# Two weight sums of a seven-product block made by accumulating loads instead of vector subtractions

## The chip, the core and the metric

The kernel runs on one core of a Trainium2 chip. The metric is the device time of one execution in microseconds (us), as a median over runs. TensorE (PE in the profile) multiplies, PEld is its weight load, VectorE is DVE, ScalarE is ACT, GpSimd is POOL, and SyncE (SP) does nothing but start transfers here. Transfers started by SP and by GpSimd go through queues of their own.

## The reference

One layer of a streaming encoder: a norm, one wide input projection, two mixers, two gated projections, an output projection with a residual sum, and a SwiGLU block, on 256 rows of 2048 in float32.

```python
h = rms_norm(x, norm_mix[l])
proj = jnp.einsum('btd,dn->btn', h, w_in[l])
...
gates = jax.nn.sigmoid(gate_logits + b_gate[l]); gate_a, gate_b = jnp.split(gates, 2, axis=-1)
...
merged = (gate_a * jnp.einsum('btc,cd->btd', y_a, w_proj_a[l])
          + gate_b * jnp.einsum('btc,cd->btd', y_b, w_proj_b[l]))
x = x + jnp.einsum('btd,de->bte', merged, w_out[l])
h = rms_norm(x, norm_ffn[l])
gate_up = jnp.einsum('btd,df->btf', h, w_ffn_in[l])
ff_gate, ff_up = jnp.split(gate_up, 2, axis=-1)
x = x + jnp.einsum('btf,fd->btd', jax.nn.silu(ff_gate) * ff_up, w_ffn_out[l])
```

The weights w_in, w_ffn_in and w_ffn_out are by far the largest arrays, and nearly all of the time is the multiplication with them.

## The kernel before

**Tiles.** A weight matrix lies in memory as blocks of 512 columns by 512 rows: a chunk `kc` of a block `nb` is four k-tiles of 128 rows, each 128 x 512 (256 KB). The 256 rows of activations are two halves, m = 0 and 1. Each operand is split into a high part in float32r and the rest: `hi = copy(w)` on ScalarE, `lo = w - hi` on VectorE. A product is then a triple of matmuls, hi x hi, hi x lo and lo x hi, into one bank. A plain product of one chunk and one block is 4 k-tiles by 2 halves, 8 triples; of a pair of blocks, 16.

**Seven products.** For some chunks of some pairs of blocks, `product_pair` handles the first two k-tiles of the chunk, the two halves of the rows and the two blocks as a 2 x 2 by 2 x 2 block product with seven products instead of eight; the other two k-tiles go plainly, with 8 triples. Such a chunk is called a use here: 7 + 8 = 15 triples. There are 46 uses: four in each of two gate pairs (`SEVEN_GATE`), four in one pair of the output projection (`SEVEN_OUT`), four in each of five FFN pairs (`SEVEN_IN`), and seven (`SEVEN`) of the eleven chunks in each of the two pairs of the last product. Four sums of weights are needed: `weight_forms` makes two of them in `ta` and two in `tb`, each 128 x 512, by four vector instructions, all from line 194 of the profile. `act_forms` makes the four sums of activations; `four_sums` and `residual_sums` put the products together.

**Stages of a weight.** A `fetch` loads two tiles of two k-tiles (512 KB each) from SP's queue into the pool `wraw` of 8 buffers. `halves` splits one raw tile into a `hi` and a `lo` tile, of which there are 4 each; ScalarE and VectorE can thus prepare at most four tiles ahead of TensorE. `ta` and `tb` both come from the pool `t6` of 2 buffers. Within a use the preparation goes: first raw tile, the single k-tile of the second, `ta`, `tb`, then the two raw tiles of the plain part (`early` uses, the first chunk of a product with `plain_first`, have the plain part first). 

**Order.** Loads and splits are traced with a priority 500 instructions ahead (`PREP_AHEAD`). The order of the instructions on each engine is fixed when the program is built, by a list scheduler that works with modelled durations, priorities and free buffers; at run time each engine takes its instructions in that order and waits on semaphores. TensorE's order is as written. Side work (transposes, mixers) comes in through `tick`, every four triples. GpSimd has little to do: loads and stores of `x` and of spilled activation forms, the gate additions of line 809, and small powers for the norms.

Of the kernel before, what the change touches and what calls it, by code (L numbers as in the profile page):

```python
# [10 lines left out]
F32 = mybir.dt.float32  # L11
# [34 lines left out]
def block_kernel(ctx: ExitStack, tc: tile.TileContext, x, x_t, w_in, w_pa, w_pb, w_out, w_fi, w_fo,  # L46
# [51 lines left out]
    def add(out, a, b):  # L98
        nc.vector.tensor_tensor(out=out, in0=a, in1=b, op=ALU.add)

    def rsqrt_mean(dst, ss, n):

        w = ss.shape[-1]
        ms = t_small([P, 8], "ms")
        nc.vector.tensor_scalar(ms[:, :w], ss, 1.0 / n, EPS, ALU.mult, ALU.add)
        nc.gpsimd.tensor_tensor(out=dst, in0=ms[:, :w], in1=neg_half[:, :w], op=ALU.pow)
# [17 lines left out]
    def fetch(w, nb, kc, n=2, pinned=False):  # L124

        res = []
        for hf in range(2):
            raw = wraw_p.tile([P, 2, 512], F32, tag="raw", name=nm("raw"))
            for k in range(0, 2, n):
                d = nc.sync.dma_start(out=raw[:, k:k + n, :],  # L130
                                      in_=w[nb, kc, :, 2 * hf + k:2 * hf + k + n, :])
                if pinned:
                    tc.keep_in_program_order(d)
            res.append(raw)
        return res

    def load_weights(w, nb, kc, n=2, raw=None):

# [46 lines left out]
        split(hi[:, 0:n, :], lo[:, 0:n, :], src)  # L185
        return [(hi[:, k, :], lo[:, k, :]) for k in range(n)]

    def weight_forms(r0, r1):


        ta = t6_p.tile([P, 2, 512], F32, tag="t6", name=nm("ta"))
        tb = t6_p.tile([P, 2, 512], F32, tag="t6", name=nm("tb"))
        b11, b21, b12, b22 = r0[:, 0, :], r0[:, 1, :], r1[:, 0, :], r1[:, 1, :]
        op = lambda out, x, y, o: nc.vector.tensor_tensor(out=out, in0=x, in1=y, op=o)  # L194
        p1, p2 = halves(r0)
        p3, = halves(r1[:, 1:2, :])
        op(ta[:, 0, :], b12, b11, ALU.subtract)
        op(ta[:, 1, :], b22, b12, ALU.subtract)
        p5, p7 = halves(ta)
        op(tb[:, 0, :], ta[:, 0, :], b22, ALU.subtract)  # L200
        op(tb[:, 1, :], b21, tb[:, 0, :], ALU.add)
        p6, p4 = halves(tb)
        return {1: p1, 2: p2, 3: p3, 4: p4, 5: p5, 6: p6, 7: p7}

    def product_pair(w, nbs, n_chunks, act, forms, c_pool, u_pool, epilogue, plain_first=False,
                     last=False):

        tag = {id(mm): "mm", id(aux): "bank"}  # L210
        cb, ub = {}, {}
        count = [0]

        def bank_of(d, key, pool):
            if key not in d:
                d[key] = pool.tile([P, 512], F32, tag=tag[id(pool)], name=nm("mp"))
                return d[key], True
            return d[key], False

        def triple(psb, a, b, final):  # L220
            (ps, first), (ah, al), (wh, wl) = psb, a, b
            nc.tensor.matmul(ps, lhsT=ah, rhs=wh, start=first, stop=False)  # L222
            nc.tensor.matmul(ps, lhsT=ah, rhs=wl, start=False, stop=False)  # L223
            nc.tensor.matmul(ps, lhsT=al, rhs=wh, start=False, stop=final)  # L224
            count[0] += 1
            if count[0] % 4 == 0:
                tick()

        def seven(kc, tf):
            sf = forms[kc]  # L230
            form = {5: 0, 6: 1, 7: 2, 3: 3}
            plain = {1: (0, 0), 2: (1, 0), 4: (1, 1)}
            dest = {2: (0, 0), 3: (0, 1), 4: (1, 0)}
            for p in (1, 2, 3, 5, 7, 6, 4):
                if p in form:
                    a = (sf[:, 0, form[p], :], sf[:, 1, form[p], :])
                else:
                    k, m = plain[p]
                    a = act(kc * 4 + k, m)
                if p in dest:  # L240
                    triple(bank_of(cb, dest[p], c_pool), a, tf[p], False)
                else:
                    triple(bank_of(ub, p, u_pool), a, tf[p], kc == max(forms))
            if kc == max(forms):
                epilogue(ub)

        for kc in range(n_chunks):
            end = kc == n_chunks - 1
            early = plain_first and kc == 0
            with tc.high_priority(offset=min(PREP_AHEAD, tc.cur_priority - first_block[0])):  # L250
                r = [fetch(w, nb, kc) for nb in nbs]
                ws = [[None] * 4 for _ in nbs]
                if kc not in forms:
                    for n in range(2):
                        ws[n][0:2] = halves(r[n][0])
                        ws[n][2:4] = halves(r[n][1])
                else:
                    if not early:
                        tf = weight_forms(r[0][0], r[1][0])
                    for n in range(2):  # L260
                        ws[n][2:4] = halves(r[n][1])
                    if early:
                        tf = weight_forms(r[0][0], r[1][0])
            if kc in forms and not early:
                seven(kc, tf)
            ks = [k for k in range(4) if ws[0][k] is not None]
            order = [(n, k, m) for n in range(2) for k in ks for m in range(2)]
            if last and end:
                order = [(n, k, m) for n in range(2) for m in range(2) for k in ks]
            for n, k, m in order:  # L270
                triple(bank_of(cb, (m, n), c_pool), act(kc * 4 + k, m), ws[n][k], end and k == 3)
            if kc in forms and early:
                seven(kc, tf)
        return cb
# [42 lines left out]

    def act_forms(pt, f, gain=None):

        s = t2([P, 4, P], "sf")  # L320
        a11, a21, a12, a22 = (pt[:, k, m * P:(m + 1) * P] for k in range(2) for m in range(2))

        def op(out, x, k, y, o):
            if gain is None:
                nc.vector.tensor_tensor(out=out, in0=x, in1=y, op=o)
            else:
                nc.vector.scalar_tensor_tensor(out=out, in0=x, scalar=gain[:, k:k + 1], in1=y,
                                               op0=ALU.mult, op1=o)

        if gain is None:  # L330
            nc.scalar.copy(s[:, 2, :], a21)
        else:
            nc.scalar.activation(s[:, 2, :], a21, AF.Copy, scale=gain[:, 0:1])
        op(s[:, 0, :], a22, 1, s[:, 2, :], ALU.add)
        op(s[:, 2, :], a11, 0, s[:, 2, :], ALU.subtract)
        op(s[:, 1, :], a11, 0, s[:, 0, :], ALU.subtract)
        op(s[:, 3, :], a12, 1, s[:, 1, :], ALU.add)
        split(f[:, 0], f[:, 1], s)

    def picker(tiles):  # L340
# [406 lines left out]
    def four_sums(ub, e00, e10, e01, e11):  # L747

        nc.scalar.copy(e00, ub[1])
        add(e01, ub[6], e00)  # L750
        add(e10, ub[7], e01)
        add(e11, ub[5], e10)
        add(e01, ub[5], e01)

    def x_forms():

# [10 lines left out]
    for nb in range(4):  # L767
# [13 lines left out]
        if nb in SEVEN_GATE:  # L781
            def sums(ub):
                for br in range(2):
                    gates[br, nb] = t4([P, 2, 512], "gate")
                four_sums(ub, *(gates[br, nb][:, m, :] for br in range(2) for m in range(2)))

            cb = product_pair(w_in, (14 + nb, 18 + nb), 4, act_x, fq, aux, mm, sums,
                              plain_first=True, last=True)
            for br in range(2):
                gt = gates[br, nb]  # L790
                for m in range(2):
                    add(gt[:, m, :], cb[m, br], gt[:, m, :])
                    nc.vector.scalar_tensor_tensor(out=gt[:, m, :], in0=gt[:, m, :],
                                                   scalar=r1[:, m:m + 1], in1=bgs[br],
                                                   op0=ALU.mult, op1=ALU.add)
                    nc.scalar.activation(gt[:, m, :], gt[:, m, :], AF.Sigmoid)
# [23 lines left out]
    def residual_sums(x0, x1):  # L820
        def sums(ub):
            u2, u3 = t2([P, 512], "u2"), t2([P, 512], "u3")
            add(x0[:, 0, :], x0[:, 0, :], ub[1])
            nc.scalar.copy(u2, ub[1])
            add(u2, ub[6], u2)
            add(u3, ub[7], u2)
            add(x1[:, 0, :], x1[:, 0, :], u2)
            add(x0[:, 1, :], x0[:, 1, :], u3)
            add(x1[:, 1, :], x1[:, 1, :], u3)
            for m in range(2):  # L830
                add(x1[:, m, :], ub[5], x1[:, m, :])
        return sums

    def norm_block(nb, ps):
# [30 lines left out]
    def swiglu_pair(j):  # L865
# [7 lines left out]
        cb = product_pair(w_fi, (j, NJ + j), 4, act_x2, fx, aux, mm, sums, plain_first=True,  # L873
                          last=True)
        for m in range(2):
            add(hn[:, m, :], cb[m, 0], hn[:, m, :])
            nc.scalar.activation(hn[:, m, :], hn[:, m, :], AF.Silu, scale=r2[:, m:m + 1])
        for m in range(2):
            add(u[m], cb[m, 1], u[m])
# [110 lines left out]
```

## Time and profile before

| | us |
|---|---|
| median of 3 runs | 1428.48 |
| lowest and highest run | 1426.71, 1428.92 |
| the profiled execution | 1427.22 |
| its span, first to last instruction | 1425.4 |
| PE busy in the span | 1417.6 |
| DVE busy | 1063.6 |
| ACT busy | 774.2 |
| POOL busy | 50.1 |

The profile is of one execution. Its span leaves out 1.8 us that lie around the first and the last instruction. Busy times are unions of an engine's instructions; a busy PE can still be waiting inside a matmul, so the pace from matmul to matmul is read beside it.

### The profile page before, as it was taken

How to read it: one execution, taken by the hardware profiler on the slowest of the kernel's cores; microseconds unless marked ns; L12 is line 12 of the kernel's file. 1: busy time of each engine (PE TensorE's matmuls, PEld its weight loads, DVE VectorE, ACT ScalarE, POOL GpSimd, SP SyncE). 2: the span in 40 equal slices, each digit the busy share in tenths (PEclk: the TensorE clock that was granted, in tenths of full speed). 3: DMA queues.
4: the chain of work that ended last, by engine and by line, in shares of the span. 5: the costliest groups of instructions: out<-in, count | busy, mean ns of one | idle time of the engine just before them, and what ended most of it. 6: DMA issues, size and time to landing. Idle time of an engine off the chain costs nothing.

```text
span 1425.4 us, 17596 instructions
## 1 busy us (share of the span) xinstructions
PE 1417.6 (99%) x6448; PEld 1174.4 (82%) x6448; DVE 1063.6 (75%) x1361; ACT 774.2 (54%) x1009; POOL 50.1 (4%) x63
## 2 busy tenths in 40 slices
PE   9999999999999999999999999999999999999998
PEld 7888888888888888878888888888788888888887
DVE  6768869564878697689767769687796876777875
ACT  7756565555655454455555546455454554544553
POOL 0100100100000000100000000000000010000000
PEclk9999999999999999999999999999999999999999
DMA  9654354446657556547654657656476578666652
GB/s 360 243 192 161 134 193 156 164 163 195 222 183 240 197 197 210 184 148 239 220 203 168 228 169 240 206 179 228 164 238 206 178 254 303 210 221 221 208 183 84
DMA packets 81848, 288.37 MB, mean 202 GB/s; under 512 B 9185, under 2 KB 9441, under 8 KB 81761
## 3 DMA queue, kind: packets, MB, share of 16 engines
q1 hardware_dynamic: 78272, 274.66, 57.5%
q0 software_dynamic: 3488, 12.58, 2.3%
q8 instruction: 50, 0.82, 0.2%
q14 instruction: 38, 0.30, 0.1%
HBM read 279.34 MB, written 7.86 MB: 201 GB/s over the span
## 4 chain that ended last, share of the span: by engine, by line
PE 98%; DVE 1%; ACT 0%; DMA 0%; issue 0%; SPq 0%; DVEq 0%; ACTq 0%
PE mm L169 18%; PE mm L168 18%; PE mm L170 18%; PE mp L223 13%; PE mp L224 13%; PE mp L222 13%; PE bank L285 2%; PE bank L543 1%; DVE wlo L178 1%; ACT whi L177 0%; PE bank L573 0%; DMA raw<-in_w_in 0%; PE bank L619 0%; PE bank L670 0%; PE bank L698 0%; DVE tb L194 0%
## 5 line engine op out<-in xcount | busy, mean ns | idle before, releaser
L148 DVE TENSOR_TENSOR wlo<-raw,whi 128x1024 fp32r<-128x1024 f32 (+1 forms) x292 | 351.9, 1212 | 175.6 <-ACT whi L147 173.4
L147 ACT CAST whi<-raw 128x1024 fp32r<-128x1024 f32 (+1 forms) x292 | 301.9, 1040 | 292.7 <-PE mm L170 219.8
L178 DVE TENSOR_TENSOR wlo<-raw,whi 128x1024 fp32r<-128x1024 f32 x216 | 235.0, 1110 | 51.9 <-ACT whi L177 50.8
L177 ACT CAST whi<-raw 128x1024 fp32r<-128x1024 f32 x216 | 201.2, 960 | 121.8 <-PE mp L224 59.6
L168 PE MATMUL mm<-whi,xTh 128*128 128x512 f32 x576 | 226.6, 398 | 1.3 <-ACT whi L147 1.3
L169 PE MATMUL mm<-wlo,xTh 128*128 128x512 f32 x576 | 225.2, 391 | 0.0
L170 PE MATMUL mm<-whi,xTl 128*128 128x512 f32 x576 | 225.1, 391 | 0.0
L168 PE MATMUL mm<-whi,x2Th 128*128 128x512 f32 x384 | 150.0, 391 | 0.0
L170 PE MATMUL mm<-whi,x2Tl 128*128 128x512 f32 x384 | 149.5, 389 | 0.0
L169 PE MATMUL mm<-wlo,x2Th 128*128 128x512 f32 x384 | 149.4, 389 | 0.0
L168 PEld LDWEIGHTS mm<-whi,xTh 128*128 128x128 f32 x576 | 108.2, 188 | 23.0 <-ACT whi L147 2.0
L170 PEld LDWEIGHTS mm<-whi,xTl 128*128 128x128 f32 x576 | 108.2, 188 | 22.6
L169 PEld LDWEIGHTS mm<-wlo,xTh 128*128 128x128 f32 x576 | 108.3, 188 | 21.8 <-DVE wlo L148 1.0
L223 PE MATMUL mp<-wlo,hTh 128*128 128x512 f32 x282 | 109.7, 389 | 0.0
L224 PE MATMUL mp<-whi,hTl 128*128 128x512 f32 x282 | 109.6, 389 | 0.0
L222 PE MATMUL mp<-whi,hTh 128*128 128x512 f32 x282 | 99.7, 390 | 0.0
L177 ACT CAST whi<-ta 128x1024 fp32r<-128x1024 f32 x46 | 48.3, 1050 | 89.9 <-PE mp L224 87.4
L178 DVE TENSOR_TENSOR wlo<-ta,whi 128x1024 fp32r<-128x1024 f32 x46 | 56.2, 1223 | 48.3 <-ACT whi L177 48.3
L224 PE MATMUL mp<-whi,x2Tl 128*128 128x512 f32 x220 | 86.2, 392 | 0.0
L223 PE MATMUL mp<-wlo,x2Th 128*128 128x512 f32 x220 | 86.2, 392 | 0.0
L170 PEld LDWEIGHTS mm<-whi,x2Tl 128*128 128x128 f32 x384 | 72.1, 188 | 15.0
L168 PEld LDWEIGHTS mm<-whi,x2Th 128*128 128x128 f32 x384 | 72.1, 188 | 14.8
(256 smaller groups left out, 2260.8 us busy)
## 6 DMA issues: line engine op xcount, KB each, us to landing
raw<-in_w_fi SPq DMA_DIRECT2D x176, 512.0 KB, 4.4
raw<-in_w_in SPq DMA_DIRECT2D x172, 512.0 KB, 4.1
raw<-in_w_fo SPq DMA_DIRECT2D x88, 512.0 KB, 5.3
raw<-in_w_out SPq DMA_DIRECT2D x32, 512.0 KB, 4.3
raw<-in_w_pa SPq DMA_DIRECT2D x16, 512.0 KB, 3.7
raw<-in_w_pb SPq DMA_DIRECT2D x16, 512.0 KB, 4.3
x<-x POOLq DMA_DIRECT2D x8, 512.0 KB, 5.7
kept<-sform POOLq DMA_DIRECT2D x7, 512.0 KB, 4.9
```

The lines of the kernel that those rows point to most:

```text
L147: nc.scalar.copy(hi[:, sl, :], src[:, sl, :])
L148: nc.vector.tensor_tensor(out=lo[:, sl, :], in0=src[:, sl, :], in1=hi[:, sl, :].bitcast(F32), op=ALU.subtract)
L168: nc.tensor.matmul(ps[m], lhsT=ah, rhs=wh, start=kc == 0 and k4 == 0, stop=False)
L169: nc.tensor.matmul(ps[m], lhsT=ah, rhs=wl, start=False, stop=False)
L170: nc.tensor.matmul(ps[m], lhsT=al, rhs=wh, start=False, stop=kc == n_chunks - 1 and k4 == 3)
L177: nc.scalar.copy(hi, src)
L178: nc.vector.tensor_tensor(out=lo, in0=src, in1=hi.bitcast(F32), op=ALU.subtract)
L222: nc.tensor.matmul(ps, lhsT=ah, rhs=wh, start=first, stop=False)
L223: nc.tensor.matmul(ps, lhsT=ah, rhs=wl, start=False, stop=False)
L224: nc.tensor.matmul(ps, lhsT=al, rhs=wh, start=False, stop=final)
L285: nc.tensor.transpose(out=pt[:, j, m * P:(m + 1) * P], in_=nat[:, m, c:c + P], identity=ident)
L543: nc.tensor.matmul(pl[:, j, :], lhsT=ek[:, g // 2, (g % 2) * P:(g % 2 + 1) * P], rhs=eq[:, g, :], start=True, stop=True)
```

## The change

A use no longer fetches its first two k-tiles as two plain raw tiles. `fetch_pair` loads the first k-tile of both blocks into the two halves of a raw tile `ta`, and GpSimd's queue then starts a load of the second block's first two k-tiles into the same tile with an addition (`accum_op`), so that `ta` holds two sums when it lands. It must wait for the two loads. The plain values needed beside it are loaded into two more raw tiles, `b1` and half of `b22`; the plain part's two raw tiles stay as they were. A use thus takes five raw tiles of the eight instead of four. `weight_forms` makes only the two sums of `tb`. All four sums of weights are now additions, so some signs of the products change, and `act_forms`, `four_sums`, `residual_sums` and the callers of the results add where they subtracted and the other way round, with the same number of instructions.

```diff
+    def fetch_pair(w, nbs, kc):
+        ta = raw_tile()
+        for n in range(2):
+            nc.sync.dma_start(out=ta[:, n, :], in_=w[nbs[n], kc, :, 0, :])
+        nc.gpsimd.dma_start(out=ta, in_=w[nbs[1], kc, :, 0:2, :], accum_op=ALU.add)
+        b1, b22 = raw_tile(), raw_tile()
+        nc.sync.dma_start(out=b1, in_=w[nbs[0], kc, :, 0:2, :])
+        nc.sync.dma_start(out=b22[:, 1, :], in_=w[nbs[1], kc, :, 1, :])
+        rest = []
+        for nb in nbs:
+            rest.append(raw_tile())
+            nc.sync.dma_start(out=rest[-1], in_=w[nb, kc, :, 2:4, :])
+        return (ta, b1, b22), rest
...
-    def weight_forms(r0, r1):
-        ta = t6_p.tile([P, 2, 512], F32, tag="t6", name=nm("ta"))
+    def weight_forms(ta, b1, b22):
         tb = t6_p.tile([P, 2, 512], F32, tag="t6", name=nm("tb"))
-        b11, b21, b12, b22 = r0[:, 0, :], r0[:, 1, :], r1[:, 0, :], r1[:, 1, :]
-        op = lambda out, x, y, o: nc.vector.tensor_tensor(out=out, in0=x, in1=y, op=o)
-        p1, p2 = halves(r0)
-        p3, = halves(r1[:, 1:2, :])
-        op(ta[:, 0, :], b12, b11, ALU.subtract)
-        op(ta[:, 1, :], b22, b12, ALU.subtract)
+        p1, p2 = halves(b1)
+        p3, = halves(b22[:, 1:2, :])
         p5, p7 = halves(ta)
-        op(tb[:, 0, :], ta[:, 0, :], b22, ALU.subtract)
-        op(tb[:, 1, :], b21, tb[:, 0, :], ALU.add)
+        add(tb[:, 0, :], ta[:, 0, :], b22[:, 1, :])
+        add(tb[:, 1, :], b1[:, 1, :], tb[:, 0, :])
         p6, p4 = halves(tb)
...
-        if gain is None:
-            nc.scalar.copy(s[:, 2, :], a21)
-        else:
-            nc.scalar.activation(s[:, 2, :], a21, AF.Copy, scale=gain[:, 0:1])
-        op(s[:, 0, :], a22, 1, s[:, 2, :], ALU.add)
-        op(s[:, 2, :], a11, 0, s[:, 2, :], ALU.subtract)
-        op(s[:, 1, :], a11, 0, s[:, 0, :], ALU.subtract)
-        op(s[:, 3, :], a12, 1, s[:, 1, :], ALU.add)
+        nc.scalar.activation(s[:, 3, :], a21, AF.Copy, scale=1.0 if gain is None else gain[:, 0:1])
+        op(s[:, 0, :], a22, 1, s[:, 3, :], ALU.subtract)
+        op(s[:, 2, :], a11, 0, s[:, 3, :], ALU.subtract)
+        op(s[:, 1, :], a11, 0, s[:, 0, :], ALU.add)
+        op(s[:, 3, :], a12, 1, s[:, 1, :], ALU.subtract)
...
-        add(e01, ub[6], e00)
-        add(e10, ub[7], e01)
-        add(e11, ub[5], e10)
-        add(e01, ub[5], e01)
+        sub(e01, ub[6], e00)
+        sub(e10, e01, ub[7])
+        sub(e11, e10, ub[5])
+        sub(e01, e01, ub[5])
```

`residual_sums` and the three places that add the results of a pair get the same kind of edit: a `sub` with the same operands where an `add` stood.

## Rows read from the trace of the kernel before

**Rows 1.** The page's first part: busy us, share of the span, instructions.
```profile
span 1425.4 us, 17596 instructions
...
PE 1417.6 (99%) x6448; PEld 1174.4 (82%) x6448; DVE 1063.6 (75%) x1361; ACT 774.2 (54%) x1009; POOL 50.1 (4%) x63
```

**Rows 2.** The page's chain that ended last, shares by engine.
```profile
PE 98%; DVE 1%; ACT 0%; DMA 0%; issue 0%; SPq 0%; DVEq 0%; ACTq 0%
```

**Rows 3.** Windows: stretch, its length, each engine's busy us, PE clock, DMA share, GB/s.
```profile
0.00:36.00 36.00, 33.53 (x135) 26.41 (x136) 23.64 (x44) 25.58 (x48) 1.76 (x9) 1.00 0.95 361
...
505.00:545.00 40.00, 40.00 (x178) 33.04 (x177) 37.12 (x45) 23.28 (x27) 0.00 (x0) 1.00 0.66 225
...
900.00:940.00 40.00, 40.00 (x182) 33.12 (x181) 25.27 (x32) 19.06 (x23) 0.53 (x1) 1.00 0.56 184
...
1400.00:1425.00 25.00, 21.41 (x95) 17.41 (x93) 15.78 (x20) 7.65 (x8) 0.00 (x0) 1.00 0.11 42
```

**Rows 4.** Timeline of PE inside a use: start us, us, instruction (first and last of nine).
```profile
1249.67 0.39 PE L224 MATMUL mp<-whi,hTl 128*128 128x512 f32 x1
...
1251.48 0.39 PE L224 MATMUL mp<-whi,hTl 128*128 128x512 f32 x1
```

**Rows 5.** Waits of PE's weight loads: us in total, times, longest.
```profile
PEld mp L222 <- ACT whi L177: 3.2, 6, 1.0
PEld mp L223 <- DVE wlo L178: 2.5, 7, 0.5
```

**Rows 6.** The line of the weight sums: ns min/median/max, first and last start.
```profile
L194 DVE TENSOR_TENSOR ta<-raw,raw x46: 682/691/996, 387.6 to 1387.3; 128x512 f32<-128x512 f32 x46
L194 DVE TENSOR_TENSOR ta<-raw x46: 680/685/689, 388.2 to 1387.9; 128x512 f32<-128x512 f32 x46
```

**Rows 7.** Timeline of DVE in the last product, two successive uses.
```profile
1242.34 1.23 DVE L178 TENSOR_TENSOR wlo<-ta,whi 128x1024 fp32r<-128x1024 f32 x1 [2.45 <-ACT whi L177]
1243.60 0.69 DVE L194 TENSOR_TENSOR ta<-raw,raw 128x512 f32<-128x512 f32 x1
1244.20 0.69 DVE L194 TENSOR_TENSOR ta<-raw 128x512 f32<-128x512 f32 x1
...
1252.99 1.22 DVE L178 TENSOR_TENSOR wlo<-ta,whi 128x1024 fp32r<-128x1024 f32 x1 [1.26 <-ACT whi L177]
...
1255.76 1.22 DVE L178 TENSOR_TENSOR wlo<-tb,whi 128x1024 fp32r<-128x1024 f32 x1 [0.21 <-ACT whi L177]
```

**Rows 8.** DMA issues: out<-in, engine, count, KB each, median us to landing.
```profile
raw<-in_w_fo SPq DMA_DIRECT2D x88, 512.0 KB, 5.3
...
raw<-in_w_pa SPq DMA_DIRECT2D x16, 512.0 KB, 3.7
...
x<-x POOLq DMA_DIRECT2D x8, 512.0 KB, 5.7
kept<-sform POOLq DMA_DIRECT2D x7, 512.0 KB, 4.9
sf<-kept POOLq DMA_DIRECT2D x7, 512.0 KB, 10.1
raw<-in_w_in SPq DMA_DIRECT2D x8, 256.0 KB, 6.2
...
bg<-in_b_gate SPq DMA_DIRECT2D x8, 256.0 KB, 4.5
```

**Rows 9.** Timeline of ACT at the same crossing.
```profile
1254.67 1.05 ACT L177 CAST whi<-tb 128x1024 fp32r<-128x1024 f32 x1 [1.72 <-PE mp L224]
```

**Rows 10.** All waits: who waited for whom, us in total, times, longest.
```profile
DVE ta L194 <- DMA raw<-in_w_fi: 8.2, 4, 2.3
```

**Rows 11.** Timeline of POOL: the last gate additions.
```profile
623.22 3.00 POOL L809 TENSOR_TENSOR gate<-gate,gate 128x512 f32<-128x512 f32 x2 [19.29 <-DVE gate L808]
```

**Rows 12.** The tile bank after them: weight loads of its transposes, ns, first and last start.
```profile
L285 PEld LDWEIGHTS bank<-ident,gate x8: 138/138/141, 628.5 to 631.0; 128*128 128x128 f32 x8
```

More of the change, by code (lines that the diff above doesn't have):

```diff
@@ L99, in add, with sub @@
         nc.vector.tensor_tensor(out=out, in0=a, in1=b, op=ALU.add)
+    def sub(out, a, b):
+        nc.vector.tensor_tensor(out=out, in0=a, in1=b, op=ALU.subtract)
     def rsqrt_mean(dst, ss, n):
@@ L127, in fetch @@
         for hf in range(2):
-            raw = wraw_p.tile([P, 2, 512], F32, tag="raw", name=nm("raw"))
+            raw = raw_tile()
             for k in range(0, 2, n):
@@ L135, in fetch, with raw_tile @@
         return res
+    def raw_tile():
+        return wraw_p.tile([P, 2, 512], F32, tag="raw", name=nm("raw"))
+    def fetch_pair(w, nbs, kc):
[11 more added lines that the diff above has]
+        return (ta, b1, b22), rest
     def load_weights(w, nb, kc, n=2, raw=None):
@@ L250, in product_pair @@
             with tc.high_priority(offset=min(PREP_AHEAD, tc.cur_priority - first_block[0])):
-                r = [fetch(w, nb, kc) for nb in nbs]
                 ws = [[None] * 4 for _ in nbs]
                 if kc not in forms:
+                    r = [fetch(w, nb, kc) for nb in nbs]
                     for n in range(2):
@@ L257, in product_pair @@
                 else:
+                    r, rest = fetch_pair(w, nbs, kc)
                     if not early:
-                        tf = weight_forms(r[0][0], r[1][0])
+                        tf = weight_forms(*r)
                     for n in range(2):
-                        ws[n][2:4] = halves(r[n][1])
+                        ws[n][2:4] = halves(rest[n])
                     if early:
-                        tf = weight_forms(r[0][0], r[1][0])
+                        tf = weight_forms(*r)
             if kc in forms and not early:
@@ L791, in block_kernel @@
                 for m in range(2):
-                    add(gt[:, m, :], cb[m, br], gt[:, m, :])
+                    (sub if (m, br) == (1, 0) else add)(gt[:, m, :], cb[m, br], gt[:, m, :])
                     nc.vector.scalar_tensor_tensor(out=gt[:, m, :], in0=gt[:, m, :],
@@ L824, in sums @@
             nc.scalar.copy(u2, ub[1])
-            add(u2, ub[6], u2)
-            add(u3, ub[7], u2)
+            sub(u2, ub[6], u2)
+            sub(u3, u2, ub[7])
             add(x1[:, 0, :], x1[:, 0, :], u2)
-            add(x0[:, 1, :], x0[:, 1, :], u3)
+            sub(x0[:, 1, :], x0[:, 1, :], u3)
             add(x1[:, 1, :], x1[:, 1, :], u3)
             for m in range(2):
-                add(x1[:, m, :], ub[5], x1[:, m, :])
+                sub(x1[:, m, :], x1[:, m, :], ub[5])
         return sums
@@ L875, in swiglu_pair @@
         for m in range(2):
-            add(hn[:, m, :], cb[m, 0], hn[:, m, :])
+            (sub if m == 1 else add)(hn[:, m, :], cb[m, 0], hn[:, m, :])
             nc.scalar.activation(hn[:, m, :], hn[:, m, :], AF.Silu, scale=r2[:, m:m + 1])
```

## Prediction

> **What bounds the kernel now.** I read the first lines of the page first: TensorE has work in 1417.6 us of a span of 1425.4 us [rows 1]. The chain of waits says the same of the end: 98% of it is PE [rows 2]. So the next question is what the missing 7.8 us are. The windows put 2.47 us of them into the first 36 us (36.00 - 33.53) and 3.59 us into the last 25 (25.00 - 21.41), where weights first arrive and results leave [rows 3]; neither stretch is touched by the change. About 1.7 us are left for everything between. In a stretch full of uses, as in a plain one, TensorE is busy without a gap (40.00 of 40) at a granted clock of 1.00, its level of 2.4 GHz [rows 3]. Its pace is even: from 1249.67 to 1251.48 it starts nine matmuls, one each 0.226 us [rows 4]. The change issues the same matmuls, so **no version of it gains more than some 2 us**, 0.1%, which is under what can be measured: a time within 0.2% (2.9 us) of the old one counts as no change.
>
> The vector engine is what the change relieves, and it is close to full in the uses: 37.12 us of 40, against 25.27 of 40 in a plain stretch [rows 3]. Still PE's weight loads waited for it 2.5 us in all, seven times [rows 5]. That is the stall that the change can remove; the views show no larger one.
>
> **What goes.** Each of the 46 uses loses two subtractions of 128x512 on VectorE, 691 and 685 ns alone and some 0.6 us each where they follow one another [rows 6, 7]: 46 x 2 x 0.6 = 55 us of VectorE. They are off the chain, so this is worth at most the 2.5 us of that wait, with those of ACT beside it [rows 5]; I take 1.5 us, under the 1.7 us found above. The rewritten signs (add for sub, scaled activation for copy) keep the count, engine and shape of every instruction, so I cost them at nothing. They hide under the pace of TensorE, and VectorE has more room than before.
>
> **What comes.** Before, a use fetched four tiles of 512 KB. Now it fetches 2 x 256 (ta), 512 (accumulating, from GpSimd's queue), 512, 256 and 2 x 512 KB, 2816 KB in place of 2048: 768 KB more, two more issues on SP's queue and one on GpSimd's. A use is 15 triples of matmuls, 45 x 0.226 = 10.2 us. The added bytes are 77 GB/s in that time. The stretch of uses moved 225 GB/s at a share of 0.66 [rows 3]; with 302 GB/s the share is 0.66 x 302/225 = 0.89. If the accumulating transfer also has to read its 512 KB of destination, that is another 51 GB/s and a share of 1.04 by the same scaling, 0.93 by that of the opening (0.95 at 361 GB/s). So the transfers come near their limit, but only for four uses at a time or three in the last product; plain chunks between them want much less (0.56) [rows 3]. I take the throughput as just enough and charge its effect to latency.
>
> The rows show GpSimd's 512 KB landing later than SP's (5.7 us beside 3.7 to 5.3) [rows 8], but not why. The Trainium skill (DMA: Bandwidth & Descriptors, section Issuing engines are not separate DMA queues) says that transfers started from different engines run on the same 16 DMA engines, so that GpSimd's queue brings no bandwidth of its own. By that rule the addition is paid in the share above and the second rival below has its reason; if it did not hold, the share would stay near 0.74 (0.66 x 251/225, with 256 KB more) and that rival would go. No row of before shows an accumulating transfer, so the trace leaves it open.
>
> **The new chain** is what decides. A use's ta was two vector instructions; now it is load, wait on GpSimd, accumulating load. The loads: 256 KB took 4.5 us on SP's queue in mid-kernel (the gate bias) and 6.2 us in the crowded opening; 512 KB took 3.7 to 5.3 us [rows 8]. The trace of before has no accumulating transfer. Its cost is bounded by GpSimd's transfers of 512 KB: 4.9 us (store of forms), 5.7 us (x) and 10.1 us (seven at once) [rows 8]. Low end 3.7 + 4.9 = 8.6 us, high end 6.2 + 10.1 = 16.3 us. Nearest rows: 4.5 + 5.7 = 10.2 us; a second reading of 512 KB at the opening's 361 GB/s adds 1.45 us. **I take 11.7 us.** The Trainium skill's fit for GpSimd's transfers (DMA: Bandwidth & Descriptors, section Anatomy of one DMA: 2.0 us plus bytes over 436 GB/s) would put the accumulating part at 3.2 us by my estimate and the chain at 7.7 us, the first rival below; the rows of 512 KB show more, and the sum goes by them.
>
> **What it must fit into.** There are 8 raw tiles and a use now takes 5, so ta's loads can be issued when the third tile of the use two earlier is released, which is when VectorE ends wlo<-ta of that use. In the last product that is 1242.34 + 1.23 = 1243.57 for the use whose successor's wlo<-ta starts at 1252.99 [rows 7]. The next question is where the two remaining additions (tb) stand in VectorE's order. That order is fixed when the program is built, by when the data is expected; an instruction that waits holds everything behind it. Before, ta needed a t6 buffer that came free only after wlo<-ta, and so it stood right behind it [rows 7]; ta has now left that pool, and the additions can stand earlier.
>
> TensorE crosses into the new use at about 1254.6: the cast of tb, which waits for the last tile of the old use, starts at 1254.67 [rows 9]. P1 to P3 are nine matmuls, so the wlo half of ta is wanted at 1254.6 + 10 x 0.226 = 1256.9, and must start by 1255.65. Two additions take 1.29 us. If they stand **ahead of wlo<-ta**, the accumulated tile must have landed by 1254.36, 10.8 us after the loads' issue. If they stand **ahead of wlo<-tb** (wanted six matmuls later, 1258.2, start by 1257.0), by 1255.7, 12.1 us after. Behind that it would be some 13.5 us or more. The chain of 11.7 us is 0.9 us late in the first place and in time in the second. 32 of the 46 uses follow directly on another use (3 in each of 8 products of four, 4 in each of the last two). I put half in each place: 16 x 0.9 = 14.4 us. The other 14 follow a plain chunk, where VectorE already stood waiting for a load up to 2.3 us [rows 10] without TensorE waiting; the cover there is two or three prepared tiles of 12 matmuls (2.7 us each), and I cost them at nothing. If that cover were gone they cost the same 0.9 us each, 13 us.
>
> One more wait: on GpSimd the accumulating load stands in order with the gate additions (3.00 us for the last pair at 623.22), whose transposes load at 628.5 [rows 11, 12], 2.3 us after they end. An accumulating load of the output projection that stands ahead and waits longer for its tile than this stalls TensorE once; at most one landing, some 5 us. I take nothing, since ta's loads are issued long before in that stretch of plain chunks.
>
> **Sum.** Against the profiled execution's 1427.22 us (1.3 us under the median): 1427.2 + 14.4 - 1.5 = 1440.1; with the 1.3 us, **1441 us**.
>
> **Rivals.**
> First, **not slower: the chain is hidden.** If ta lands within 10.8 us, which the low end (8.6) and the nearest rows without the second reading (10.2) give, or if all additions stand late, nothing waits. Then TensorE's pace sets 1425.5 to 1428.5 us. For it: PE waits almost nowhere now, and VectorE gets 1.2 of each 10.2 us back in the uses. Against it: transfers will be slower than those rows, with the share near 1. Chance 0.40.
> Second, **the accumulating transfer is slow or the DMA engines fill.** At 10.1 us for it the chain is 14.6 us, 3.8 and 2.5 us too late in the two places; 32 x 3.1 = 100 us, 1527 us. A share of 1.04 alone costs 0.04 x 10.2 x 46 = 19 us. Time 1460 to 1530. For it speak the shares worked out above; against it, that buffered tiles carry four uses. Chance 0.13.
> Third, **faster by over 0.2%**: would need more stall than the 1.7 us that the windows leave. Chance 0.04.
> The forecast, late by a fraction of a microsecond to some two in a use, 1431 to 1460 us, has 0.43, hardly more than the hidden case: the price of being late is paid in every use, and the sum has the chain on the wrong side of the nearer place.
>
> **How the numbers follow.** Faster 0.04, same 0.40, slower 0.43 + 0.13 = 0.56. The forecast's own range is 1431 to 1460 us. For 8 in 10 the range takes in the hidden case below and the start of the second rival above: 1425 to 1475 us.
>
> **What the profile after would show.** Right: groups of tb additions on VectorE that wait for the DMA of ta, PE's weight loads waiting for wlo in the uses, TensorE's idle time up by some 14 us, DMA share in the uses near 0.9. Wrong: additions that start without a wait and PE idle still near 8 us (hidden case); an accumulating load that lands after 10 us or more, or a share of 1.0 over a whole product (second rival). The sum would be wrong in its first term if the additions stand elsewhere than the two places, and in its size if the accumulating load's landing is far from 7 us.

## The result, and the profile after

The changed kernel takes 1617.83 us (median of 4 runs, 1616.8 to 1622.4) beside 1427.7 us before (median of 4): a ratio of 1.134, 95% interval 1.131 to 1.136. The prediction had the direction, slower; 190 us more lie far outside its range of 1425 to 1475 us. The profiled execution took 1622.4 us.

The page after: the span, busy us of the engines, the two large DMA queues, the chain that ended last.

```profile
span 1620.6 us, 17925 instructions
...
PE 1484.6 (92%) x6448; PEld 1214.6 (75%) x6448; DVE 1007.0 (62%) x1269; ACT 774.5 (48%) x1009; POOL 90.3 (6%) x109
...
q1 hardware_dynamic: 91520, 286.72, 53.7%
q0 software_dynamic: 10112, 36.70, 10.5%
...
PE 4%; DMA 2%; DVE 1%; issue 0%; ACT 0%; DVEq 0%; SPq 0%; POOLq 0%
```

VectorE lost 1063.6 - 1007.0 = 56.6 us of work, as worked out (55). TensorE, which had 7.8 us without work [rows 1], now has 1620.6 - 1484.6 = 136.0, and its busy time itself grew by 67.0 us with the same 6448 matmuls. The chain no longer runs through PE [rows 2]; it follows back to a short tail and names no bound, so the waits must.

Waits after: who waited for whom, us in total, times, longest.

```profile
DVE tb L99 <- DMA raw<-in_w_fi: 123.0, 20, 9.9
DVE tb L99 <- DMA raw<-in_w_fo: 81.4, 13, 10.0
DVE tb L99 <- DMA raw<-in_w_in: 50.9, 7, 9.0
DVE tb L99 <- DMA raw<-in_w_out: 25.4, 4, 8.5
...
PEld mp L240 <- DVE wlo L200: 146.1, 38, 7.5
PE mp L240 <- DVE wlo L200: 130.2, 33, 7.0
```

In 44 of 46 uses the first tb addition stands on VectorE and waits for ta, 280.7 us in all. TensorE then waits for a `wlo` half 130.2 us: that is the growth of its idle time (136.0 - 7.8 = 128.2). Before, weight loads waited 2.5 us [rows 5]. Each of the 32 uses that follow another has one of these 33 gaps behind its addition; of the other 14, one has a gap of 0.22 us.

The windows show how the rest arises, in the same columns as [rows 3]: a stretch of uses, and a short one behind a single gap.

```profile
505.00:545.00 40.00, 31.66 (x122) 24.97 (x121) 19.27 (x21) 14.47 (x16) 2.60 (x3) 0.87 0.66 183
...
1060.00:1075.00 15.00, 12.41 (x44) 10.05 (x45) 9.56 (x10) 4.79 (x6) 0.00 (x0) 0.77 0.54 175
```

Timeline of PE in that short stretch: start us, us, instruction, idle before it and what ended that.

```profile
1062.59 0.79 PE L240 MATMUL mp<-wlo,fx 128*128 128x512 f32 x1 [5.00 <-DVE wlo L200]
1063.18 0.63 PE L241 MATMUL mp<-whi,fx 128*128 128x512 f32 x1
...
1067.02 0.63 PE L241 MATMUL mp<-whi,x2Tl 128*128 128x512 f32 x1
...
1070.77 0.39 PE L241 MATMUL mp<-whi,x2Tl 128*128 128x512 f32 x1
1071.00 0.39 PE L239 MATMUL mp<-whi,x2Th 128*128 128x512 f32 x1
```

After 5.00 us without work the ten matmuls from 1063.18 to 1067.02 start 0.43 us apart (3.84 / 9), against 0.23 us at 1070.77, the pace of before [rows 4]: TensorE is at its lower level of 1.2 GHz there, and the window's granted clock is 0.77, where the windows of before have 1.00 [rows 3]. So a gap costs its own length (3.9 us in the mean of the 33) and then about 2 us of slow matmuls: 67.0 us over 33 gaps.

Where it is lost: set against before matmul by matmul, each of the eight products of four uses took 12.1 to 20.5 us more (146 in all), and the last two products 20.2 and 28.4; the other products took nothing more.

### The profile page after: what moved, and what is told of

It reads as the page before. It is cut to its first block, busy times and chain, and to the rows that moved or that the text cites. A ratio compares the mean times of both kernels' runs of the same rounds, so it can differ in the third digit from the quotient of the medians.

```text
span 1620.6 us, 17925 instructions
## 1 busy us (share of the span) xinstructions
PE 1484.6 (92%) x6448; PEld 1214.6 (75%) x6448; DVE 1007.0 (62%) x1269; ACT 774.5 (48%) x1009; POOL 90.3 (6%) x109
## 3 DMA queue, kind: packets, MB, share of 16 engines
q0 software_dynamic: 10112, 36.70, 10.5%
## 5 line engine op out<-in xcount | busy, mean ns | idle before, releaser
L170 DVE TENSOR_TENSOR wlo<-raw,whi 128x1024 fp32r<-128x1024 f32 (+1 forms) x292 | 349.9, 1210 | 164.6 <-ACT whi L169 162.2
L169 ACT CAST whi<-raw 128x1024 fp32r<-128x1024 f32 (+1 forms) x292 | 302.1, 1040 | 292.3 <-PE mm L192 213.7
L199 ACT CAST whi<-raw 128x1024 fp32r<-128x1024 f32 (+1 forms) x262 | 250.4, 975 | 349.4 <-PE mp L241 273.5
L200 DVE TENSOR_TENSOR wlo<-raw,whi 128x1024 fp32r<-128x1024 f32 (+1 forms) x262 | 288.1, 1132 | 90.5 <-ACT whi L199 90.5
L99 DVE TENSOR_TENSOR tb<-raw,raw 128x512 f32<-128x512 f32 x46 | 31.8, 692 | 280.7 <-DMA raw<-in_w_fi 123.0
L240 PE MATMUL mp<-wlo,x2Th 128*128 128x512 f32 x220 | 96.1, 437 | 35.4 <-DVE wlo L200 35.4
L239 PE MATMUL mp<-whi,hTh 128*128 128x512 f32 x282 | 103.6, 403 | 0.0
L241 PE MATMUL mp<-whi,x2Tl 128*128 128x512 f32 x220 | 93.9, 427 | 0.0
L239 PE MATMUL mp<-whi,x2Th 128*128 128x512 f32 x220 | 84.6, 427 | 0.0
L240 PEld LDWEIGHTS mp<-wlo,x2Th 128*128 128x128 f32 x220 | 46.3, 210 | 49.3 <-DVE wlo L200 39.7
```

What stands on the lines that cost most here:

```text
L169: nc.scalar.copy(hi[:, sl, :], src[:, sl, :])
L170: nc.vector.tensor_tensor(out=lo[:, sl, :], in0=src[:, sl, :], in1=hi[:, sl, :].bitcast(F32), op=ALU.subtract)
L199: nc.scalar.copy(hi, src)
L200: nc.vector.tensor_tensor(out=lo, in0=src, in1=hi.bitcast(F32), op=ALU.subtract)
```

## The loop in the trace after, read from one product

Timeline after, VectorE in one product of four uses.

```profile
1111.45 0.69 DVE L99 TENSOR_TENSOR tb<-raw,raw 128x512 f32<-128x512 f32 x1 [4.82 <-DMA raw<-in_w_fi]
1112.18 0.69 DVE L99 TENSOR_TENSOR tb<-raw,tb 128x512 f32<-128x512 f32 x1
1112.79 4.68 DVE L170 TENSOR_TENSOR wlo<-raw,whi 128x1024 fp32r<-128x1024 f32 x4
...
1130.05 0.69 DVE L99 TENSOR_TENSOR tb<-raw,raw 128x512 f32<-128x512 f32 x1 [9.86 <-DMA raw<-in_w_fi]
1130.78 0.69 DVE L99 TENSOR_TENSOR tb<-raw,tb 128x512 f32<-128x512 f32 x1
1131.39 2.35 DVE L200 TENSOR_TENSOR wlo<-raw,whi 128x1024 fp32r<-128x1024 f32 x2
...
1145.67 0.69 DVE L99 TENSOR_TENSOR tb<-raw,raw 128x512 f32<-128x512 f32 x1 [4.68 <-DMA raw<-in_w_fi]
...
1150.74 1.23 DVE L200 TENSOR_TENSOR wlo<-tb,whi 128x1024 fp32r<-128x1024 f32 x1 [0.51 <-ACT whi L199]
```

Timeline after, SP's queue in the same stretch (L148 is the pair of loads of ta, L156 the two plain tiles).

```profile
1115.17 0.80 SPq L148 DMA_DIRECT2D raw<-in_w_fi  x2
...
1120.22 12.74 SPq L156 DMA_DIRECT2D raw<-in_w_fi  x2
1133.77 0.81 SPq L148 DMA_DIRECT2D raw<-in_w_fi  x2
```

And GpSimd, which starts the accumulating load.

```profile
1122.29 0.86 POOL L149 DMA_DIRECT2D raw<-in_w_fi  x1 [17.86 <-DMA raw<-in_w_fi]
```

Read in order: ta's loads are issued at 1115.17, GpSimd adds to them from 1122.29, and the addition that stood on VectorE since 1120.19 starts at 1130.05, 14.9 us after the issue. While it stood, SP's queue stood too: the second load of L156 needs a raw tile, which VectorE lets go only with the splits behind the addition (1131.39 and after). SP's own waits say the same for the whole run (us in total, times, longest):

```profile
SPq L156 <- DVE wlo L200: 223.9, 73, 12.1
```

So the next ta is issued at 1133.77, **behind** the addition of the use before, and its own addition starts at 1145.67. The tb of 1130 is not split before 1150.74: there was no hurry.

That is a loop: addition, splits, free raw tiles, next loads, accumulating load, next addition. Of the 46 uses I took the 24 that follow another inside a product of four. From the issue of ta's loads to the addition: 14.0 us in the mean. From the addition of the use before to these loads: 4.1 us (3.0 to 7.5). One turn takes 18.1 us, and TensorE needs 10.2 us a use.

The places fall from 9 halves ahead in the first use of such a product to 6 in the last (counted as in the next section), so the order itself sets the additions further apart than 10.2 us. In each of the eight products the splits between the first addition and the last feed 153 matmuls, in place of the 135 of three uses: 153 x 0.226 = 34.6 us, 11.5 us a turn. Three turns thus lose 3 x (18.1 - 11.5) = 19.8 us by this estimate; the products of four lost 18.3 in the mean (146 / 8).

## The experiments

The theories, as the expectations name them. A: the additions stand too early in VectorE's fixed order, and their wait holds what is behind them. B: the accumulating load, or the bytes added, is too slow wherever the additions stand. C: the signs or what else was rewritten. D: the early place costs something by itself. E (last two): there are too few raw tiles. "Halves ahead" counts the `wlo` halves that VectorE splits between a use's additions and the split of their result; in the changed kernel it is 6 to 9 in 45 uses and 3 in one. The diffs are against the changed kernel.

**The place, five ways.** Nothing but the place of the two additions is edited; loads, bytes and queues stay.

```diff
-        add(tb[:, 0, :], ta[:, 0, :], b22[:, 1, :])
-        add(tb[:, 1, :], b1[:, 1, :], tb[:, 0, :])
+        with tc.issue_after(behind.ins):
+            add(tb[:, 0, :], ta[:, 0, :], b22[:, 1, :])
+            add(tb[:, 1, :], b1[:, 1, :], tb[:, 0, :])
```

`behind` is the VectorE split of ta (0 halves ahead):

> The changed kernel, with the two additions of each use put behind the split of ta of the same use in VectorE's order; nothing else is edited. Theory A (the additions stand 6 to 9 weight halves too early in VectorE's fixed order, and what is queued behind them waits with them): the 281 us that they wait for the accumulating load go, TensorE's idle time falls from 136 us to under 20, the granted clock returns to 1.00, 1427 to 1440 us. Theory B (the accumulating load or the added bytes are too slow for the pace, wherever the additions stand): ta itself is then late for its split, and the time stays over 1550 us.

of b22 (1 half):

> The additions one half earlier than in e1, behind the split of b22 of the same use. Theory A: the accumulating load has been landed for longer than the 17 us that this place leaves it in nearly all uses, so 1427 to 1440 us as in e1, perhaps a few us less, since the split of tb then has more time. Theory B: over 1550 us.

of b1 (2 halves):

> The additions two weight halves ahead of the split of tb (behind the split of b1), where the run behind b22 had them one ahead. Theory A, by place: the loads-to-landing chain of some 13.7 us (11 to 19) still ends before this place in most uses, and the cast of tb no longer waits for the additions, so 1427 to 1433 us, at or just under the run behind b22. If the chain's tail is already late here, 1433 to 1440 us.

of the last tile before the use (3 halves):

> The additions three halves ahead of the split of tb (behind the last half prepared before this use's own). Theory A: some 18 us from the loads' issue to this place against a chain of 13.7 us, so most uses in time, 1428 to 1440 us.

and two splits earlier (5 halves in 37 uses; 9 in seven, the first of a product; 3 and 4 in the other two):

> The additions five halves ahead of the split of tb in all uses but the first of a product of four (those nine ahead, as in the changed kernel). Theory A: the place leaves some 13 us, the chain of 13.7 us (11 to 19) is late by about 1 us in the middle and 3 to 5 us in its tail, in 37 uses, so 1450 to 1530 us, between the run behind b22 and the changed kernel's 1618. If instead early additions cost by something other than the wait (buffers held, order of the rest), the time has no reason to rise with the place and stays near 1432 or jumps to 1600.

| halves ahead | us | ratio to before, 95% | wait of the additions for DMA, us | PE busy of span |
|---|---|---|---|---|
| 0 | 1479.49 | 1.035 (1.033 to 1.038) | 0 | 1436.1 of 1468.2 |
| 1 | 1432.23 | 1.0022 (1.0013 to 1.0031) | 13.6 | 1420.4 of 1430.6 |
| 2 | 1428.97 | 1.0000 (0.9991 to 1.0009) | 17.7 | 1417.5 of 1428.0 |
| 3 | 1429.13 | 1.0003 (0.9993 to 1.0014) | 37.2 | 1418.2 of 1426.9 |
| 5 | 1489.21 | 1.043 (1.038 to 1.047) | 130.5 | 1435.8 of 1480.8 |
| 6 to 9 (the change) | 1617.83 | 1.134 (1.131 to 1.136) | 280.7 | 1484.6 of 1620.6 |

The whole loss is gone two or three halves ahead. With five, TensorE waits again:

```profile
PE mp L244 <- DVE wlo L200: 37.7, 17, 5.4
```

All 17 waits come behind additions at five halves, none behind the seven at nine, which stand at the entry of a product.

Windows of the kernel with 2 halves, the columns as in [rows 3]:

```profile
505.00:545.00 40.00, 40.00 (x178) 33.11 (x177) 34.78 (x40) 23.50 (x26) 0.86 (x1) 1.00 0.86 280
1100.00:1150.00 50.00, 50.00 (x226) 41.42 (x226) 39.47 (x44) 27.83 (x31) 1.76 (x2) 1.00 0.85 251
```

The same 505 to 545 us as in [rows 3]: TensorE full again, DMA share up from 0.66 to 0.86 at 280 GB/s, close to the 0.89 at 302 that the prediction scaled. B falls. The Trainium skill (DMA: Bandwidth & Descriptors, section Issuing engines are not separate DMA queues) has GpSimd's transfers on the same engines as SP's. The trace agrees: the share of these engines rose with them to 0.86, where the prediction put 0.74 if that did not hold.

In this kernel ta's loads are issued 8.6 us in the mean **before** the additions of the use before (24 of 24 times before, after the change 24 of 24 behind). One such place in its timelines of SP and VectorE; the loads at 1109.24 are those of the addition at 1124.73:

```profile
1109.24 0.85 SPq L148 DMA_DIRECT2D raw<-in_w_fi  x2
...
1117.10 0.69 DVE L99 TENSOR_TENSOR tb<-raw,raw 128x512 f32<-128x512 f32 x1
...
1124.73 0.69 DVE L99 TENSOR_TENSOR tb<-raw,raw 128x512 f32<-128x512 f32 x1
```

The loop is open, and the additions follow one another 10.2 us apart in the mean.

With 0 halves ahead the expectation (1427 to 1440 us) missed, and the loss is another one. Waits of that kernel:

```profile
ACT whi L199 <- DVE tb L99: 94.5, 37, 3.2
...
PEld mp L242 <- ACT whi L199: 40.1, 43, 2.3
...
PE mp L242 <- ACT whi L199: 22.4, 39, 1.9
```

Now the additions come too late for the cast of tb on ScalarE, which waits for them 94.5 us in 37 uses, and TensorE waits for the cast. The right place has an edge on both sides.

**The signs alone.** The fetch of before and all four sums on VectorE, as additions.

```diff
+        ta = t6_p.tile([P, 2, 512], F32, tag="t6", name=nm("ta"))
+        add(ta[:, 0, :], b1[:, 0, :], b22[:, 0, :])
+        add(ta[:, 1, :], b22[:, 0, :], b22[:, 1, :])
...
-                    r, rest = fetch_pair(w, nbs, kc)
+                    r = [fetch(w, nb, kc) for nb in nbs]
```

> Only the rewritten signs: all four sums of weights as additions, but all four made on VectorE from the four raw tiles of the kernel before. Theory A and theory B both: the time of before within 0.2% (1425 to 1431 us). Theory C (the rewritten signs moved the order of the work and cost part of the loss): over 1435 us.

Measured: 1429.13 us, ratio 1.0001 (0.9993 to 1.0010), PE 1417.7 us busy of a span of 1425.5. C falls.

**A plain load in place of the accumulating one.**

```diff
-        nc.gpsimd.dma_start(out=ta, in_=w[nbs[1], kc, :, 0:2, :], accum_op=ALU.add)
+        nc.gpsimd.dma_start(out=ta, in_=w[nbs[1], kc, :, 0:2, :])
```

> The accumulating load replaced by a plain load of the same bytes on the same queue into the same tile, so that two of the four sums are missing from the result; everything else as in the changed kernel. Theory A: the load lands some 2 us sooner (about 5.8 us in place of 7.9) and the additions still stand too early, so 1500 to 1560 us. Theory B, the accumulation itself is what is slow: 1425 to 1440 us.

Measured: 1529.4 us, ratio 1.070 (1.068 to 1.073). The line of GpSimd's loads of ta, time from issue to landing, of the changed kernel:

```profile
DMA to landing us min/median/max: 5.4/7.9/10.5
```

The same line of this kernel:

```profile
DMA to landing us min/median/max: 3.9/5.8/9.3
```

And its queue on the page, where the change shows 10.5%:

```profile
q0 software_dynamic: 10112, 36.70, 7.1%
```

For the same bytes on the same queue the accumulation costs 2.1 us. The Trainium skill's fit for GpSimd's transfers (DMA: Bandwidth & Descriptors, section Anatomy of one DMA), 3.2 us by the estimate in the prediction, is under both; the measurement decides. The chain from the issue of ta's loads to their full landing has here a median of 11.7 us, the very figure that the prediction used, and yet the kernel is 101 us slower than before. So the accumulation, with its longer chain and its larger share of the DMA engines, explains 88 us of the change's loss, and what the prediction made of a chain of 11.7 us was wrong too. The loop says why: chain to addition 11.8 + 4.1 back to the next loads = 15.9 us a turn, still over the 11.5 of the order.

**The addition at its early place, without the wait for ta.** It reads a half of b1 in place of one of ta.

```diff
-        add(tb[:, 0, :], ta[:, 0, :], b22[:, 1, :])
+        add(tb[:, 0, :], b1[:, 0, :], b22[:, 1, :])
```

> The changed kernel with the first of the two additions reading b1's first half instead of ta, so that one of the four sums lacks a term; the additions may stand as early as before and nothing that VectorE does ahead of the split of ta waits for the accumulating load, which is still issued and still read by that split. Theory A: no wait, so 1427 to 1440 us. Theory D (the early place costs by itself, by the buffers of tb and raw that it holds): over 1500 us.

Measured: 1431.67 us, ratio 1.0022 (1.0011 to 1.0032). Waits of this kernel:

```profile
DVE tb L99 <- DMA raw<-in_w_fi: 39.4, 17, 4.7
...
PE mp L240 <- DVE wlo L200: 4.7, 8, 1.0
```

The additions still wait 88.4 us in all (this row and those of the other arrays), for b1 and b22, and TensorE hardly notices. D falls: the place costs only with a wait that is long enough. A turn is 12.9 us here (8.8 + 4.1), where the order of this kernel sets 11.3; three turns of a product lose 3 x 1.6 = 4.8 us, and nearly all of it is covered (the span is 1431.1, 5.7 more than before, over all products). After the change only 1.5 us a product (19.8 - 18.3) are covered. What covers it, tiles prepared ahead as the prediction took it, is argued, not shown.

**More and fewer raw tiles.** The loop says that a buffer more or less changes little, since the order places the additions by the same buffers. For nine tiles the pool `t2` went from 3 to 2.

```diff
-    wraw_p = ctx.enter_context(tc.tile_pool(name="wraw", bufs=8))
+    wraw_p = ctx.enter_context(tc.tile_pool(name="wraw", bufs=9))
-    t2_p = ctx.enter_context(tc.tile_pool(name="t2", bufs=3))
+    t2_p = ctx.enter_context(tc.tile_pool(name="t2", bufs=2))
```

> The changed kernel with nine raw tiles in place of eight (room for it comes from two t2 tiles in place of three). With the ninth tile the fixed order on VectorE puts the additions a half earlier too, 7 to 11 halves ahead of the split of their tile, so the loads of ta and the additions that wait for them move together. Theory A, as a loop (additions hold VectorE, VectorE holds the raw tiles, the tiles hold the loads of the next ta, and these hold the next additions): in the changed kernel the loads of ta are issued 4.1 us after the additions of the use before began (mean of the 24 transitions inside the eight products of four uses, all between 3.0 and 7.5) and the additions can start 14.0 us later, 18.1 us a use where the matmuls need 10.2. The ninth tile leaves the loop closed, so it stays near 18 us a use and the kernel at 1570 to 1630 us. Rival E, too few buffers: a tile more lets each load of ta start some 2 to 3 us earlier against the work of TensorE, and the loss falls by a third to a half: 1520 to 1560 us.

With `bufs=7` in the first pool and nothing else:

> The changed kernel with seven raw tiles in place of eight. The fixed order then puts the additions later, 2 to 9 halves ahead, most of them one or two less than with eight. Theory A as a loop: the loads of ta still follow the additions of the use before by some 4 us and the loop stays near 17 to 18 us a use in the products of four; the last two products, where the places fall to 4 to 7, lose less: 1560 to 1620 us. Rival E, too few buffers: a tile less starts each load of ta 2 to 3 us later and the loss grows by a third or more: above 1680 us.

Measured: 1593.42 us with nine (ratio 1.117, 1.114 to 1.120) and 1590.65 us with seven (1.114, 1.112 to 1.116). A turn takes 17.7 us with nine (14.2 + 3.5) and 17.8 us with seven (13.7 + 4.1). Both kernels lie in what the loop gave and outside what E gave. Each is some 25 us faster than the change with eight; for seven the places, one or two halves later in most uses, go with it, for nine the turn is 0.4 us shorter. Why they are that much faster was not settled, and the nine-tile kernel has a `t2` tile less as well. More raw tiles with the additions held in their place were not tried.

## Why the prediction was wrong, point by point

- **No gain is to be had: right.** Two and three halves ahead give the change its best case, with 55 us less work on VectorE, and the time is that of before, TensorE busy 1417.5 and 1418.2 us against 1417.6 [rows 1]. The 1.5 us that the sum took off are not seen.
- **Signs and removed instructions at nothing: right** (the signs alone, 1.0001).
- **Direction and mechanism: right in kind.** Additions that wait for ta's DMA, weight loads that wait for `wlo`: both are in the waits, as the prediction said they would be. DMA share near 0.9 shows only where nothing waits (0.86); after the change it is 0.66, since all went slower.
- **The first term of the sum, "16 x 0.9 = 14.4 us", is the step that failed.** It measured 1620.6 - 1425.4 = 195.2 us, 6.1 us for each of the 32 uses that follow another. Three parts of it were wrong:
  1. *What it must fit into.* The prediction set the chain against a timetable of before: ta's loads at 1243.57, the addition wanted by 1254.36, late once by 0.9 us. But lateness moves the timetable: the loads of the next ta wait for tiles whose splits stand behind the waiting addition. The right comparison is of a turn (chain and way back, 18.1 us) with the matmuls that the order puts between two additions (11.5 us). The plain load takes part 3 away, with the very chain of 11.7 us, and 101 us are still lost to this part and the next; no run parts these two.
  2. *Where the additions stand.* I gave half of the uses the place ahead of `wlo<-ta` of the use before (7 halves ahead) and half a later one, ahead of `wlo<-tb` (6), at no cost. 30 of 46 stand at 7 or more, 26 of them at 8 or 9. With the measured chain a place of 5 loses and 2 and 3 do not, so the later of my two was too early as well.
  3. *The chain.* 14.0 us to the addition in the products of four, against 11.7: the accumulating load took 7.9 us for 7.15, the loads and the start on GpSimd (0.7 us after they land) the rest. It was inside the bounds (8.6 to 16.3). The seven loads behind the high bound's 10.1 us were not issued at once, as the prediction has it, but from 1164.70 to 1180.12; the sum did not use them.
- **A term was missing:** the clock. 67.0 of the 195.2 us are TensorE's own busy time, slow matmuls behind gaps. How much of it would stay with fewer, longer gaps was not tried.
- **The 14 uses behind a plain chunk at nothing: held.** In seven of the eight products of four the first addition waits 3.6 to 5.6 us on VectorE, in the first of them not at all, and TensorE loses nothing there; the other six cost it one gap of 0.22 us.
- **The gate additions on GpSimd at nothing: held.** After the change the last of them ran from 671.23 us for 2.96 us between two accumulating loads (658.20 and 677.16), and no matmul of its transposes (from 675.38) waited.
- **The second rival** named a slow accumulating load or full DMA engines, 1527 us at a chain of 14.6. The chain came close; its price of 3.1 us a use was again lateness counted once, and the engines were not full (share 0.66). None of the cases listed reached past 1530 us: the loop was in none of them, so that the direction came right is no credit for the size.
- **The first rival, hidden,** is what the same transfers do once the additions stand two or three halves ahead.

## What to carry to other kernels

When a value that an engine made itself is to come by DMA, look first for the instruction that reads it: an engine with a fixed order stands at that instruction, and if it is also the engine that frees the buffers of the loads, the wait feeds itself. Compare one turn of that loop (issue, landing, consumer, buffer free, next issue) with the work of the bounding engine that the order puts between two consumers, not one arrival with one deadline. If the turn is longer, move the consumer behind the work that frees the buffers (here 1.13 became 1.00 with no other edit); more buffers need not help, since an order made from them can move the consumer too, as the ninth tile did here. And relieving an engine that is off the critical path bought nothing here, though 55 us of its work went.

## What the runs showed of the hardware

An accumulating load of 512 KB from GpSimd's queue took 7.9 us in the median, a plain one 5.8; GpSimd was busy 862 ns with starting the first and 530 ns with the second; and the same 36.70 MB took 10.5% of the engines' time instead of 7.1%, though that span was 6% longer. A gap of 5.00 us in TensorE's work was followed by ten matmuls at half pace, and the granted clock of a whole execution with 33 gaps of 3.9 us in the mean was 0.95.
